# Keys grouped in column strips instead of row groups, and twice as many second-stage projections by the seven-product scheme

## The chip, the cores and the metric

The kernel runs on one core of a Trainium2 chip. The metric is the device time of one execution in microseconds; the time of a kernel is the median over several runs. The profile shows one execution on that core: TensorE (PE, with its weight loads as PEld), VectorE (DVE), ScalarE (ACT), GpSimd (POOL), and the queue on SyncE (SP), from which nearly all transfers are issued.

## What is computed

One layer of a neighbourhood-attention encoder over 2048 tokens of width 1024, which form a grid of 32 rows by 64 columns, with 16 heads of 64, all in float32:

```python
h = rmsnorm(x, g)
q, k, v, gate = split(h @ w_in, 4)
# each query at (row, col) sees the 8 x 16 keys of a window clipped to the grid
s = q . k / 8 + rpb[head, row offset, column offset]
o = softmax(s) . v
x = x + (o * silu(gate)) @ w_out
out = rmsnorm(x, norm_f)
```

## The kernel before

**Precision.** A float32 operand is split into a high and a low part in the reduced matmul format (`hi` and `lo`), and three products (high by high, high by low, low by high) stand for one. Splits are made in pairs, the high part by ACT and the low part by DVE.

**Projections.** `w_in` has 16 units of 256 columns, four for each of q, k, v and gate. Tokens come in four chunks of 512 (chunk c holds rows 8c to 8c+7). `stage_one` makes v for tokens 0 to 1023 (`values_of`, L531), then q, k and gate of all four unit numbers for chunks 0 and 1. It does this by `seven_products` (L411): a Strassen-like scheme that makes the 2 x 2 blocks of a unit (two halves of the columns by two chunks) from seven block products of 12 matmuls each, 84 in all, instead of 96. Its `ahead` forms the weight sums (L400) and their splits (L393 on ACT, L394 on DVE) six products ahead; `add` and `out_` (L422, L428, L430) put the blocks together from PSUM, and `give` stores them to DRAM. `stage_two` makes v for the other tokens (L531), then, again by `seven_products`, the units of `units_two` for chunks 2 and 3. All other units of chunks 2 and 3 (`halves`) are left to the generator `projections`, which makes 24 matmuls per group (`group`, L355, L357 and L359) as filler of the attention stage. When it is used up, the generator `outputs` (L1250, L1252, L1254) makes the output projection, as filler too, and after the attention.

**Attention.** `order` lists pairs of heads p by row groups T of eight query rows; each is done in two iterations, one for column blocks C = 0, 1 and one for 2, 3, with 128 queries a block (8 rows by 16 columns). `KEY_ROWS` and `KEY_COLS` give the keys a block can see: 11, 15 or 12 rows by 24 or 32 columns. Iteration i of the main loop issues, in this order: filler (`feed`, which has `amount[i]` matmuls to give and goes on for a while after the last event on ACT and DVE); `normalise(i-1)` (reciprocals on DVE L1004, scaling on POOL L1006); `turns(i-2)` (transposes L1011, copied out of PSUM by DVE L1036 and ACT L1035); `scores(i)` (L988; then maximum with the bias added on DVE L995, exponential on ACT L998); `values(i-2)` (L1056; in the second of the two iterations the product with the gate on DVE, L1070). `bias` (L970, POOL) adds mask and relative position bias for a new pair of heads or row type.

**Order of keys.** Keys of a block lie row by row. `blocks(T)` cuts them into groups of four rows: a group is 96 or 128 keys deep (72 or 96 for a last group of three rows), and a half of the queries (64 partitions) needs only those groups that its window touches. The products with the values need the values in the same order on partitions: `evac_v` stores v to `vd` in DRAM, `copy_v` (L946) copies it within DRAM into one array `vc` for each pair of heads and column block, and `load_v` (L938) loads one tile `vt` for each of the four column blocks of a pair and row group.

**Order of work.** The program is scheduled by hand: every instruction stands in the order of the source. Transfers and evacuations that may come later are put into `later` with a lag counted in matmuls (`store`, `due`). Pools have fixed numbers of buffers; `vp` (values, and landing places before) has four of 512 elements.

Of the kernel before, what the change touches and what calls it, by code (L numbers as in the profile page):

```python
# [43 lines left out]
def mask_table():  # L44
    out = []
    for t, (u0, u1) in enumerate(TYPE_ROWS):
        T = (0, 1, 3)[t]
        for c, (v0, v1) in enumerate(TYPE_COLS):
            C = (0, 1, 3)[c]
            qr = T * 8 + np.arange(8)[:, None, None, None]  # L50
            qc = C * 16 + np.arange(16)[None, :, None, None]
            kr = T * 8 + np.arange(u0, u1)[None, None, :, None]
            kc = C * 16 + np.arange(v0, v1)[None, None, None, :]
# [17 lines left out]
def build(ctx, tc, x, xr, xt, wg, rpb, w_out, n0, nf, masks, out):  # L71
# [7 lines left out]
    vd = [dram.tile([4, 4, GW, 8, 128], F32, name=f"vd{u}") for u in range(2)]  # L79
    vc = {(p, C): dram.tile([4 * (c1 - c0), 8, 128], F32, name=f"vc{p}_{C}")  # L80
          for p in range(NP) for C, (c0, c1) in enumerate(KEY_COLS)}
# [12 lines left out]
    vp = pool("vp", 4)  # L94
# [126 lines left out]
    units_two = [(k, j) for j in range(1) for k in "kqg"]  # L221
    halves = [(k, j, 1, c) for j in range(1, 4) for g in (("k", "q", "g") if j < 3 else ("k", "qg")) for c in (2, 3) for k in g]
# [98 lines left out]
    def give(kind, hp, c, t, psum=False):  # L321
# [19 lines left out]
        nc.scalar.activation(hi, t, AF.Copy)  # L341
        nc.vector.tensor_tensor(lo, t, hi.bitcast(F32), OP.subtract)
# [22 lines left out]
    def evac_v(u, t, p):  # L365
        v = ev([128, 512], F32, "v")
        nc.scalar.activation(v, p, AF.Copy, scale=rt[:, t:t + 1] if t < 8 else 1.0)
        dst = vd[u].rearrange("h r c g d -> g (r c) h d")[t // 2, t % 2 * 128:t % 2 * 128 + 128]
# [169 lines left out]
    uncopied = [[(p, C, h) for p in range(NP) for C in range(4)] for h in range(2)]  # L538

    def copies(h, n):  # L540
        for _ in range(n):
            if uncopied[h]:
                copy_v(*uncopied[h].pop(0))


    def stage_one():
        us = [(k, j) for j in range(4) for k in "kqg"]
        X1 = {f: [(xs([128, 512], F32R, "h"), xs([128, 512], F32R, "l")) for _ in range(4)]
              for f in ("B12", "B11", "B21", "B22")}
        spot = mkp([128, 3, 512], F32, "spot")  # L550
        land = {f: [p([128, n], F32, "land")[:, :512] for _ in range(4)]
                for f, p, n in (("x12", kp, 960), ("x22", qp, 512), ("x11", vp, 512))}
        land["x21"] = [spot[:, k] for k in range(3)] + [lp([128, 512], F32, "land")]
        slots = [(mp, 512)] * 6 + [(ep, 512)] * 2 + [(sp, 512)] * 2 + [(pa, 768)] * 2 + [(vp, 512)] * 4
# [23 lines left out]
        def also(n, i):  # L578
            m = n + len(us) - 1
            if m and i in (1, 3, 5):  # L580
                copies(0, 1)
# [27 lines left out]
            if n == 0:  # L609
# [16 lines left out]
                elif i == 3:  # L626
                    split_v(0, 1, 1)
                    L2["x12"] = [vp([128, 512], F32, "land") for _ in range(4)]
# [127 lines left out]
    def stage_two():  # L756
        x12, x11, x21 = L2["x12"], L2["x11"], L2["x21"]
        x22 = [qp([128, 512], F32, "land") for _ in range(4)]
        for k in range(4):
# [3 lines left out]
                 "T4": [(vp, 512)] * 4 + [(mp, 512)] * 2 + [(ep, 512)] * 2}  # L763

        def also(n, i):
            copies(1, 1)
# [21 lines left out]
        def pair(u, ts, *do):  # L788
            for b in range(4):
# [3 lines left out]
                if u and ts != (12,) and b % 2:  # L793
                    copies(1, 1)
# [167 lines left out]
    def bias(p, ty, cty):  # L962
# [3 lines left out]
        sh = lambda a: a.rearrange("p (u v) -> p u v", v=v1 - v0)  # L966
        for s in range(2):
# [3 lines left out]
                sh(t), E[p, s][:, u0 + 4:u1 + 4, v0 + 8:v1 + 8], sh(MK[0][:, m0:m0 + n]), OP.add)  # L971
# [3 lines left out]
    def scores(i):  # L975
# [5 lines left out]
        for C in cs:  # L981
# [3 lines left out]
            for m, (qq, kk) in enumerate(((qh, kh), (qh, kl), (ql, kh))):  # L985
                for s in range(2):
                    a = slice(s * 64, s * 64 + 64)
                    nc.tensor.matmul(pst[s], qq[a, qs], kk[a, :r1 - r0, c0:c1], start=(m == 0), stop=(m == 2))  # L988
# [19 lines left out]
    def turn(dst, i, C, s, blk, q0, nq):  # L1008
        g, lr, nr = blk[:3]
        w = width(C)  # L1010
        nc.tensor.transpose(dst[:nr * w], X[i, C][s][q0:q0 + nq, lr * w:(lr + nr) * w],  # L1011
                            ident[q0:q0 + nq, q0:q0 + nq])

    def split(T):
        bl = blocks(T)
        return [b for b in bl if b[4] == 128], [b for b in bl if b[4] == 64]

    def turns(i):
        p, T, cs = pairs[i]
        full, part = split(T)  # L1020
        halves_ = [full + [b for b in part if b[3] == 64 * h] for h in range(2)]
        for C in cs:
            t = PT[i, C] = pa([128, 768], F32, "pta")
            slots = t.rearrange("p (n h q) -> p h n q", h=2, q=64)
            ph = [bank(384, f"ph{h}") for h in range(2)]
            for j in range(3):
                for s in range(2):
                    for h in range(2):
                        if j < len(halves_[h]):
                            o = j * 128 + s * 64  # L1030
                            turn(ph[h][:, o:o + 64], i, C, s, halves_[h][j], 64 * h, 64)
# [364 lines left out]
```

## Time and profile before

| | us |
|---|---|
| median of 3 runs | 1085.62 (1084.97 to 1085.65) |
| the profiled execution, its own time | 1086.36 |
| its span, first to last instruction | 1084.5 |
| `seven_products` of stage one on PE, from the chain | 96.7 to 326.7 |
| `values_of` of stage two | 326.7 to 414 |
| `seven_products` of stage two and first filler | 414 to 478 |
| attention | 478 to about 1027 |

The page gives busy time, share of the span and number of instructions for each engine; matmuls overlap in the array, so that the records of PE are longer than the distance between their starts. A group of instructions is a line of the kernel with its engine, operation, tiles and shape, the count after an x, then busy us, mean ns of one, and the engine's idle time before them with what ended it. A row of the timeline has its start and length in us, and in brackets the idle time before it. Two more rows of interest, the transfers that the change takes out (KB each, median us from issue to landing):

```profile
vc<-vd SPq DMA_DIRECT2D x32, 256.0 KB, 4.4
...
vc<-vd SPq DMA_DIRECT2D x32, 192.0 KB
```

### The profile page before, as it was taken

What the parts mean: (1) busy time and instruction counts of PE and PEld (TensorE: products, weight loads), DVE (VectorE), ACT (ScalarE), POOL (GpSimd) and SP (SyncE); (2) the same over time, 40 slices, a digit from 0 to 9 for tenths busy, and PEclk for the clock granted to TensorE, in tenths of its full rate; (3) what the DMA queues carried; (4) which work ended last, traced back from release to release, by engine and by line L of the source; (5) the groups of instructions that cost most, each with busy time, mean ns of one, the idle gap of its engine ahead of it and who ended that gap; (6) DMA issues with size and microseconds to landing.
All of it is one profiled execution on the core that took longest, in us unless ns stands there. A gap on an engine that the chain in (4) does not pass through costs nothing.

```text
span 1084.5 us, 21929 instructions
## 1 busy us (share of the span) xinstructions
PE 1071.1 (99%) x7657; PEld 877.1 (81%) x7657; DVE 703.2 (65%) x1644; ACT 531.2 (49%) x1345; POOL 357.9 (33%) x474
## 2 busy tenths in 40 slices
PE   9999999999999999999999999999999999999997
PEld 6888888888888888887888888888888787888885
DVE  5376778778997535576555555664676786776643
ACT  7545334333434334346555555564576565665431
POOL 0000222312221000017545534444447656566200
PEclk9999999999999999999999999999999999999999
DMA  9633557574764366889868876886899787887442
GB/s 313 212 97 106 202 173 210 163 232 146 256 188 143 108 172 170 258 277 310 245 205 267 253 216 204 255 269 200 246 319 294 230 268 231 274 262 226 126 149 78
DMA packets 145901, 231.90 MB, mean 214 GB/s; under 512 B 13824, under 2 KB 61184, under 8 KB 145792
## 3 DMA queue, kind: packets, MB, share of 16 engines
q1 hardware_dynamic: 145648, 230.25, 68.2%
q8 instruction: 61, 1.00, 0.4%
q14 instruction: 48, 0.39, 0.1%
q10 hardware_dynamic: 144, 0.26, 0.1%
HBM read 171.73 MB, written 73.40 MB: 226 GB/s over the span
## 4 chain that ended last, share of the span: by engine, by line
PE 92%; DVE 3%; DMA 1%; ACT 1%; issue 1%; SPq 0%; POOL 0%; ACTq 0%; DVEq 0%; POOLq 0%
PE pp L411 23%; PE pv L531 16%; PE o L1056 8%; PE s L988 6%; PE pp L359 6%; PE pp L357 6%; PE pp L355 6%; PE po L1254 6%; PE po L1252 5%; PE po L1250 5%; PE ph L1011 5%; PE zp L1269 1%; DMA k_hi<-hi 1%; DMA land<-in_xt_dram 0%; DVE f L394 0%
## 5 line engine op out<-in xcount | busy, mean ns | idle before, releaser
L1006 POOL TENSOR_SCALAR x<-x,st 128x360 f32<-128x360 f32 (+5 forms) x256 | 143.0, 578 | 235.0 <-DVE st L1004 192.3
L970 POOL TENSOR_TENSOR em<-e,mk 128x480 f32<-128x480 f32 (+5 forms) x160 | 136.3, 886 | 138.3 <-DMA raw<-in_xt_dram 135.0
L998 ACT ACTIVATE x<-x,st 128x360 f32<-128x360 f32 (+5 forms) x256 | 151.8, 595 | 44.4 <-DVE st L995 44.4
L411 PE MATMUL pp<-h,f 128*128 128x512 f32 x480 | 155.4, 389 | 0.0
L430 POOL TENSOR_TENSOR tmp<-tmp,rb 128x512 f32<-128x512 f32 x36 | 58.9, 1637 | 270.6 <-DVE tmp L428 223.7
L411 PE MATMUL pp<-t,f 128*128 128x512 f32 x540 | 130.0, 390 | 0.3 <-DVE u L422 0.2
L995 DVE CUSTOM_DVE_ANT_0 x<-s,em 128x360 f32<-128x360 f32 (+5 forms) x256 | 124.0, 539 | 5.3 <-PE s L988 1.4
L411 PEld LDWEIGHTS pp<-t,f 128*128 128x128 f32 x540 | 101.2, 188 | 22.2 <-DVE u L422 1.2
L359 PE MATMUL pp<-h,w 128*128 128x512 f32 x288 | 115.1, 400 | 0.0
L357 PE MATMUL pp<-l,w 128*128 128x512 f32 x288 | 113.2, 393 | 0.0
L355 PE MATMUL pp<-h,w 128*128 128x512 f32 x288 | 113.1, 393 | 0.0
L1035 ACT ACTIVATE pta<-ph 96x256 f32<-96x256 f32 (+1 forms) x224 | 58.5, 333 | 104.3 <-PE ph L1011 104.3
L1036 DVE COPY pta<-ph 128x384 f32<-128x384 f32 (+3 forms) x128 | 60.7, 514 | 72.7 <-PE ph L1011 72.5
L411 PEld LDWEIGHTS pp<-h,f 128*128 128x128 f32 x480 | 90.1, 188 | 18.8
L1254 PE MATMUL po<-wol,gh 128*128 128x512 f32 x252 | 100.3, 398 | 0.0
L1252 PE MATMUL po<-woh,gl 128*128 128x512 f32 x252 | 98.9, 393 | 0.0
L1250 PE MATMUL po<-woh,gh 128*128 128x512 f32 x252 | 98.9, 392 | 0.0
L1056 PEld LDWEIGHTS o<-pta,vt 96*64 96x64 f32 (+2 forms) x1792 | 83.6, 137 | 17.2 <-issue 10.2
L1056 PE MATMUL o<-pta,vt 96*64 96x128 f32 (+4 forms) x1792 | 92.3, 254 | 1.4 <-DVE pta L1036 1.0
L411 PE MATMUL pp<-l,f 128*128 128x512 f32 x240 | 93.4, 389 | 0.0
L531 PE MATMUL pv<-wh,h 128*128 128x512 f32 x256 | 88.1, 390 | 0.0
L531 PE MATMUL pv<-wh,l 128*128 128x512 f32 x256 | 88.0, 389 | 0.0
(148 smaller groups left out, 1916.6 us busy)
## 6 DMA issues: line engine op xcount, KB each, us to landing
raw<-in_wg_dram SPq DMA_DIRECT2D x126, 256.0 KB, 5.1
e<-in_rpb_dram SPq DMA_DIRECT2D x54, 240.0 KB, 3.9
vt<-vc SPq DMA_DIRECT2D x64, 192.0 KB, 3.7
row<-in_xr_dram SPq DMA_DIRECT2D x32, 256.0 KB, 4.3
vd<-v SPq DMA_DIRECT2D x32, 256.0 KB, 3.0
k_hi<-hi SPq DMA_DIRECT2D x32, 256.0 KB, 2.6
k_lo<-lo SPq DMA_DIRECT2D x32, 256.0 KB, 3.8
vc<-vd SPq DMA_DIRECT2D x32, 256.0 KB, 4.4
```

The lines of the kernel that those rows point to most:

```text
L355: nc.tensor.matmul(p, wh[w, b][:, cols], hh[k, c], start=(k == 0), stop=False)
L357: nc.tensor.matmul(p, wh[w, b][:, cols], hl[k, c], start=False, stop=False)
L359: nc.tensor.matmul(p, wl[w, b][:, cols], hh[k, c], start=False, stop=(k == NK - 1))
L411: nc.tensor.matmul(B[n, P], t[:, int(m == 2), c], x[k][int(m == 1)], start=P in (1, 6, 5) and k == 0 and m == 0, stop=k == 3 and m == 2, s ...
L531: nc.tensor.matmul(ps[t], a[:, o], b, start=k == 0 and m == 0, stop=k == NK - 1 and m == 2)
L970: (nc.gpsimd if attending[0] or not s else nc.vector).tensor_tensor(sh(t), E[p, s][:, u0 + 4:u1 + 4, v0 + 8:v1 + 8], sh(MK[0][:, m0:m0 + n ...
L998: nc.scalar.activation(X[i, C][s], X[i, C][s], AF.Exp, bias=st[:, s:s + 1], scale=-1.0, accum_out=st[:, 2 + s:3 + s])
L1006: nc.gpsimd.tensor_scalar(X[i, C][s], X[i, C][s], st[:, 4 + s:5 + s], 0.5, op0=OP.mult, op1=OP.mult)
L1056: nc.tensor.matmul(o[s * 64:s * 64 + 64, C * 128 + q0:C * 128 + q0 + nq], vt[C][:k, g - g0_, s * 64:s * 64 + 64], t[:k, at:at + nq], start ...
L1250: nc.tensor.matmul(p, gh, woh[q, j], start=(i == 0), stop=False)
L1252: nc.tensor.matmul(p, gl, woh[q, j], start=False, stop=False)
L1254: nc.tensor.matmul(p, gh, wol[q, j], start=False, stop=(i == NK - 1))
```

## The change

Keys of a block are grouped into strips of eight columns by all its rows (88, 96 or 120 keys deep), three or four strips a block. So `blocks(T)` becomes `strips(C)`: which half of the queries needs a strip depends on the column block instead of the row group. The order of tokens in DRAM is changed on the host (within a row, column s x 8 + c lies at c x 8 + s), so that `load_v` gets one tile for all four column blocks of a pair and row group straight from `vd`, partition by (row, c), with the eight strips one after another. `vc` and its copies go. Masks, bias and the columns of the scores are laid out by strip; q, k and the gate are brought into or out of the new token order with strided views where they are evacuated or read. `turns` has one copy on each engine, since all strips of a block are equally deep. `vp` has two buffers of 1024 elements, of which `vh` hands out halves to the earlier stages.

`units_two` has six units instead of three, and `halves` six fewer pairs of chunk and unit; `amount` follows from this, eight matmuls more go to each of the first three iterations, and the debt that `feed` may run up is half an iteration's amount instead of 12.

```diff
-def blocks(T):
-    r0, r1 = KEY_ROWS[T]
+def strips(C):
     out = []
-    for g in range(r0 // 4, (r1 + 3) // 4):
-        halves = [h for h in range(2) if abs(2 * T + h - g) <= 1]
-        out.append((g, 4 * g - r0, min(4, r1 - 4 * g), halves[0] * 64, len(halves) * 64))
+    for s in range(KEY_COLS[C][0] // 8, KEY_COLS[C][1] // 8):
+        halves = [h for h in range(2) if abs(2 * C + h - s) <= 1]
+        out.append((s, s - KEY_COLS[C][0] // 8, halves[0] * 64, len(halves) * 64))
     return out
...
-    vp = pool("vp", 4)
+    vp = pool("vp", 2)
+    vhalf = []
+
+    def vh(shape, dt, nm):
+        if not vhalf:
+            t = vp([128, 1024], dt, nm)
+            vhalf.extend((t[:, :512], t[:, 512:]))
+        return vhalf.pop(0)
...
-    units_two = [(k, j) for j in range(1) for k in "kqg"]
-    halves = [(k, j, 1, c) for j in range(1, 4) for g in (("k", "q", "g") if j < 3 else ("k", "qg")) for c in (2, 3) for k in g]
+    units_two = [(k, j) for j in range(2) for k in "kqg"]
+    halves = [(k, j, 1, c) for j in range(2, 4) for g in (("k", "q", "g") if j == 2 else ("k", "qg")) for c in (2, 3) for k in g]
...
     def tiled(t):
-        return t.rearrange("p (r C c) -> p C r c", r=8, c=16)
+        return t.rearrange("p (r c s) -> p s r c", c=8, s=8)
     def blocked(t):
-        return t.rearrange("p (C r c) -> p C r c", r=8, c=16)
+        return t.rearrange("p (s r c) -> p s r c", r=8, c=8)
+    def by_place(t):
+        return t.rearrange("p (r c s) -> p r s c", c=8, s=8)
+    def by_column(t):
+        return t.rearrange("p (r s c) -> p r s c", s=8, c=8)
...
-        nc.scalar.activation(hi, t, AF.Copy)
-        nc.vector.tensor_tensor(lo, t, hi.bitcast(F32), OP.subtract)
+        nc.scalar.activation(by_column(hi), by_place(t), AF.Copy)
+        nc.vector.tensor_tensor(by_column(lo), by_place(t), by_column(hi.bitcast(F32)), OP.subtract)
...
-    def load_v(p, T, C):
+    def load_v(p, T):
         r0, r1 = KEY_ROWS[T]
-        g0_, g1_ = r0 // 4, (r1 + 3) // 4
-        c0, c1 = KEY_COLS[C]
-        def block():
-            VT[p, T, C] = t = vp([128, 4, 128], F32, "vt")
-            nc.sync.dma_start(t[:4 * (c1 - c0), :g1_ - g0_], vc[p, C][:, g0_:g1_])
-        return [block]
-
-    def copy_v(p, C, h):
-        must(*[("v", p // 4, t) for t in range(8 * h, 8 * h + 8)])
-        c0, c1 = KEY_COLS[C]
-        g = slice(512 * h, 512 * h + 512)
-        nc.sync.dma_start(vc[p, C].rearrange("(r c) g d -> c r (g d)", r=4)[:, :, g],
-                          vd[p // 4][p % 4].rearrange("r c g d -> c r (g d)")[c0:c1, :, g])
+        must(*[("v", p // 4, t) for t in range(r0 // 2, (r1 + 1) // 2)])
+        rows = vd[p // 4][p % 4].rearrange("(k s) d -> k s d", s=8)[8 * r0:8 * r1]
+        VT[p, T] = t = vp([128, 1024], F32, "vt").rearrange("p (s d) -> p s d", s=8)
+        nc.sync.dma_start(t[:8 * (r1 - r0)], rows)
...
-                    nc.tensor.matmul(pst[s], qq[a, qs], kk[a, :r1 - r0, c0:c1], start=(m == 0), stop=(m == 2))
+                    nc.tensor.matmul(pst[s], qq[a, qs], kk[a, :r1 - r0, c0:c1].rearrange("p r (s c) -> p s r c", c=8), start=(m == 0), stop=(m == 2))
...
             for h in range(2):
-                four = sum(b[2] == 4 for b in halves_[h])
-                k = 4 * width(C)
+                n = len(halves_[h])
                 put = (lambda o, i_: nc.scalar.activation(o, i_, AF.Copy)) if h else nc.vector.tensor_copy
-                put(slots[:k, h, :2 * four], ph[h][:k, :128 * four].rearrange("p (n q) -> p n q", q=64))
-                if four < len(halves_[h]):
-                    k = halves_[h][four][2] * width(C)
-                    put(slots[:k, h, 2 * four:2 * four + 2],
-                        ph[h][:k, 128 * four:128 * four + 128].rearrange("p (n q) -> p n q", q=64))
+                put(slots[:k, h, :2 * n], ph[h][:k, :128 * n].rearrange("p (n q) -> p n q", q=64))
...
-    amount = [early / 48] * 48 + [(384 - 30) / 18] * 18
+    first = 8
+    amount = [(early - 3 * first) / 48] * 48 + [(384 - 30) / 18] * 18
+    calm_debt = amount[0] / 2
+    for i in range(3):
+        amount[i] += first
...
-        while credit[0] > 0 or credit[0] > -12 and clock[0] - state["event"] < calm:
+        while credit[0] > 0 or credit[0] > -calm_debt and clock[0] - state["event"] < calm:
...
-        if 0 < i <= N:
-            p, T, cs = pairs[i - 1]
-            later_loads(load_v(p, T, cs[0]) + load_v(p, T, cs[1]), 0, 2)
+        if i % 2 == 0 and i < N:
+            load_v(*order[m])
```

More of the change, by code (lines that the diff above doesn't have):

```diff
@@ L78, in build @@
     sgd = [dram.tile([128, S], F32, name=f"sgd{p}") for p in range(NP)]
-    vd = [dram.tile([4, 4, GW, 8, 128], F32, name=f"vd{u}") for u in range(2)]
-    vc = {(p, C): dram.tile([4 * (c1 - c0), 8, 128], F32, name=f"vc{p}_{C}")
-          for p in range(NP) for C, (c0, c1) in enumerate(KEY_COLS)}
+    vd = [dram.tile([4, S, 128], F32, name=f"vd{u}") for u in range(2)]
     ogd = [dram.tile([128, 4, NP, 128], F32, name=f"ogd{T}") for T in range(4)]
@@ L627, in also @@
                     split_v(0, 1, 1)
-                    L2["x12"] = [vp([128, 512], F32, "land") for _ in range(4)]
+                    L2["x12"] = [vh([128, 512], F32, "land") for _ in range(4)]
                     for k in range(4):
@@ L1006, in normalise, with split @@
                 nc.gpsimd.tensor_scalar(X[i, C][s], X[i, C][s], st[:, 4 + s:5 + s], 0.5, op0=OP.mult, op1=OP.mult)
[L1008 to L1016, printed above, removed]
+    def split(C):
+        return [b for b in strips(C) if b[3] == 128], [b for b in strips(C) if b[3] == 64]
     def turns(i):
         p, T, cs = pairs[i]
-        full, part = split(T)
-        halves_ = [full + [b for b in part if b[3] == 64 * h] for h in range(2)]
+        k = 8 * (KEY_ROWS[T][1] - KEY_ROWS[T][0])
         for C in cs:
+            full, part = split(C)
+            halves_ = [full + [b for b in part if b[2] == 64 * h] for h in range(2)]
             t = PT[i, C] = pa([128, 768], F32, "pta")
@@ L1047, in values @@
         o = O[p, T]
-        g0_ = KEY_ROWS[T][0] // 4
-        vt = {C: VT.pop((p, T, C)) for C in cs}
+        vt = VT[p, T]
         for C in cs:
@@ L1065, in values @@
                 for s in range(2):
-                    product(C, s, blk, PT[i, C], 512 + s * 128 + blk[3], False, h == len(part) - 1)
+                    product(C, s, blk, PT[i, C], 512 + s * 128 + blk[2], False, h == len(part) - 1)
             del PT[i, C]
         if cs[1] == 3:
+            del VT[p, T]
             og = ev([128, 512], F32, "og")
```

53 lines of the change are left out of this document (22 added, 31 removed).

## The prediction

> **What bounds the kernel now.** I read the page's busy times and clock first, then the chain that ended last, then the matrix engine's waits, then stretches of the timeline.
>
> ```profile
> span 1084.5 us, 21929 instructions
> PE 1071.1 (99%) x7657; PEld 877.1 (81%) x7657; DVE 703.2 (65%) x1644; ACT 531.2 (49%) x1345; POOL 357.9 (33%) x474
> ...
> PEclk9999999999999999999999999999999999999999
> ...
> PE 92%; DVE 3%; DMA 1%; ACT 1%; issue 1%; SPq 0%; POOL 0%; ACTq 0%; DVEq 0%; POOLq 0%
> ```
>
> A busy PE is not yet a PE at its pace, so I look for the pace in the chain in order of time (start, length, what) and for gaps in the waits of PE from 482 us to 1025 us, the attention stage.
>
> ```profile
> 181.18 68.32 PE pp L411 x300
> 329.86 84.34 PE pv L531 x372
> ...
> PE o L1056 <- DVE pta L1036: 1.0, 3, 0.3
> PE s L988 <- DVE lo L342: 0.9, 1, 0.9
> PE s L988 <- ACT pta L1035: 0.9, 3, 0.4
> PE o L1056 <- ACT pta L1035: 0.3, 1, 0.3
> PE s L988 <- DVE y L1161: 0.2, 1, 0.2
> ```
>
> 84.34/372 is 0.227 us for one 128x512 product, and 68.32/300 is 0.228 us for those of the seven-product scheme, though each record is some 390 ns long: they overlap. In the attention stage PE waits 3.3 us in all of 543 us, and no wait names a transfer. So the kernel is a queue of PE work at full clock. An edit counts if it changes the number of 512-column products, their pace, or opens a gap.
>
> **Products removed and added.** `units_two` grows from three to six. Each of the three moved units cost 96 products by `group` (two outputs, two chunks, 24 each); by `seven_products` it costs 7 x 12 = 84.
>
> ```profile
> L355 PE MATMUL pp<-h,w 128*128 128x512 f32 x288 | 113.1, 393 | 0.0
> L411 PE MATMUL pp<-t,f 128*128 128x512 f32 x540 | 130.0, 390 | 0.3 <-DVE u L422 0.2
> ```
>
> L355, L357 and L359 go from 288 each to 192 each: 288 x 0.227 = 65.4 us leave the attention stage, where they are the filler between attention steps. 3 x 84 = 252 join L411: 252 x 0.227 = 57.2 us more in stage two. The difference is 36 products, **-8.2 us**. [...]
>
> **Transposes and products with the values.** Their counts do not change (1408 transposes, 896 products): before, the number for a pair went by the row group (20 or 24, and 24 or 32 recorded passes), now by the column block (always 22 and 28). Only the depth changes: 72, 96 or 128 becomes 88, 96 or 120.
>
> ```profile
> 650.60 0.92 PE L1011 MATMUL ph<-ident,x 64*128 64x64 f32 x24
> 652.66 1.56 PE L1056 MATMUL o<-pta,vt 128*64 128x128 f32 x32
> 659.81 0.91 PE L1011 MATMUL ph<-ident,x 64*96 64x64 f32 x24
> 661.94 1.56 PE L1056 MATMUL o<-pta,vt 96*64 96x128 f32 x32
> ```
>
> In one iteration the depth is 128, in the next 96, and the blocks last the same. Term: 0.
>
> **Scores.** L988 now reads the keys in runs of 8 columns instead of 24 or 32; no operand of before has runs so short. Nearest rows:
>
> ```profile
> L988 PE MATMUL s<-kt,qh 64*128 64x360 f32 x128 | 18.0, 346 | 0.0
> L988 PE MATMUL s<-kt,qh 64*128 64x352 f32 x64 | 11.1, 350 | 0.9 <-DVE lo L342 0.9
> ```
>
> 360 elements are 15 runs of 24, 352 are 11 runs of 32: more runs, no more time. I take 0; the other bound is a stream at half pace, and as L988 holds 6% of the chain (65 us), that is +65 us.
>
> **Vector, scalar and GpSimd work.** Three more units add 21 forms with two splits each, plus sums and outputs; 12 weight splits go on each of ACT and DVE, and the second copy of `turns` on ACT (96 instructions). DVE is nearest its limit at the end of stage one, where the scheme already runs twelve units. Windows by stretch first, then the busy time of L394 on DVE and L411 on PE up to 274.8 us, with counts:
>
> ```profile
> 269.00:298.00 29.00, 28.79 (x128) 23.48 (x127) 28.44 (x38) 11.35 (x21) 8.22 (x5) 1.00 0.79 257
> 414.00:478.00 64.00, 64.00 (x284) 52.97 (x283) 39.35 (x61) 20.44 (x36) 3.44 (x4) 1.00 0.81 251
> 501.00:618.00 117.00, 117.00 (x1112) 96.28 (x1110) 62.84 (x208) 65.06 (x205) 61.51 (x100) 1.00 0.80 252
> ...
> 0.00:274.80 274.80, 60.10 (x69) 1.00 0.60 187
> ...
> 0.00:274.80 274.80, 177.80 (x783) 146.98 (x784) 1.00 0.60 187
> ```
>
> (Columns: stretch, length, busy PE, PEld, DVE, ACT, POOL, clock, DMA share, GB/s.) Even with DVE at 28.44 of 29 us, 69 forms are done when PE is at 783/12, its 66th product: three products, 3 x 12 x 0.227 = 8.2 us in hand. Stage two loads DVE 39.35/64 = 61%. Term: 0 in both stages.
>
> The `by_place` and new `tiled` views read every eighth element, 32 bytes apart (L342's `lo`, L341's `hi`, the q outputs, `og` at L1070). The trace has only runs:
>
> ```profile
> L313 DVE TENSOR_TENSOR tmp<-pp,rb 128x512 f32<-128x512 f32 x8 | 5.5, 688 | 3.7 <-PE pp L411 3.7
> L315 DVE TENSOR_TENSOR tmp<-pp,rb 128x512 f32<-128x512 f32 x4 | 2.8, 688 | 1.2 <-PE pp L411 1.2
> L1070 DVE TENSOR_TENSOR og<-o,sgt 128x512 f32<-128x512 f32 x32 | 22.0, 687 | 4.2 <-PE pp L359 2.6 <-PE o L1056 1.1
> ```
>
> L315 reads 16-element runs at the 688 ns of the contiguous L313. I take 0 extra, and a second 0.69 us on each as the other bound. In stage one's last triple that is eight operations on DVE (four k, four q), 5.5 us, less than the 8.2 us in hand.
>
> GpSimd's `em` (L970) gets runs of 8 as well:
>
> ```profile
> L970 POOL TENSOR_TENSOR em<-e,mk 128x360 f32<-128x360 f32 x44 | 40.2, 935 | 0.0
> L970 POOL TENSOR_TENSOR em<-e,mk 128x352 f32<-128x352 f32 x15 | 13.9, 949 | 1.3 <-DVE st L995 1.3
> ```
>
> Again 15 runs cost no more than 11. POOL needs 61.51 us for the 14 iterations of 501 to 618 us, 4.4 us each; these shrink from 8.3 to about 6.9 us and still cover it.
>
> **Transfers.** Issues, with KB each and us to landing:
>
> ```profile
> vt<-vc SPq DMA_DIRECT2D x64, 192.0 KB, 3.7
> ...
> vt<-vc SPq DMA_DIRECT2D x32, 144.0 KB, 4.2
> ```
>
> The 64 copies vd to vc and the 128 loads of vt go; 32 loads of up to 480 KB come, two iterations ahead of their use. Nobody on PE waited for one, so the gain is 0 there. Does the denser stage still fit? 252 GB/s over 8.3 us are 2.1 MB an iteration; the vt loads of the first row group shrink from 2 x 192 + 2 x 144 = 672 to 352 KB in two iterations, 160 KB each, and some 6.5 fillers fewer take their weights and stores with them, about 25 KB each (estimate: 1 MB of weights per 96, 256 to 512 KB of stores per 24). That leaves 1.8 MB in 6.9 us, 257 GB/s, as now. On the SP queue a load of vt still waits for the products that free its buffer, but once in two iterations, not four times.
>
> **Shorter iterations.** The filler falls from 22 to 15.5 products an iteration, 1.48 us less cover, and unevenly: in the changed program 14 of the 48 iterations before the last row group have at most 11 fillers (down to 7), where before there were five. What has to fit beneath: maximum (L995), exponentials (L998), reciprocal (L1004), copies of the transposes (L1036, L1035), then the value products. An iteration of before with 11 fillers, on DVE and PE:
>
> ```profile
> 692.74 0.17 DVE L1004 RECIPROCAL st<-st 128x2 f32<-128x2 f32 x1 [0.54 <-ACT x L998]
> 694.43 1.02 DVE L1036 COPY pta<-ph 96x384 f32<-96x384 f32 x2 [1.52 <-PE ph L1011]
> 695.99 1.56 PE L1056 MATMUL o<-pta,vt 96*64 96x128 f32 x32
> ```
>
> The reciprocals end at 692.91, the copies start at 694.43 when PE has transposed: 1.52 us to spare, 6.7 fillers. So the point is 11 - 6.7, about 4 fillers, or 7 when one 0.69 us evacuation stands between. Seven fillers are just at the edge. Where the output's chain of small operations sits on DVE, gaps were seen:
>
> ```profile
> 855.40 0.71 PE L988 MATMUL s<-kt,qh 64*128 64x480 f32 x3 [0.45 <-ACT pta L1035]
> 890.88 1.56 PE L1056 MATMUL o<-pta,vt 96*64 96x128 f32 x32 [0.34 <-DVE pta L1036]
> ```
>
> Per short iteration the bounds are 0 (at 691 us) and 0.45 us; I take 0.17, half of the 0.34 of the one with 9 fillers: nine more of them make **+1.5 us** (0 to 14 x 0.45 = 6.3).
>
> **The start of attention.** The first pairs now have three longer iterations (`first`), and their keys are no longer those of the unit just stored.
>
> ```profile
> 494.02 0.67 PE L988 MATMUL s<-kt,qh 64*128 64x352 f32 x4 [0.94 <-DVE lo L342]
> 495.14 1.33 PE L1056 MATMUL o<-pta,vt 96*64 96x128 f32 x24 [0.29 <-DVE pta L1036]
> ```
>
> At most 1.2 us go; I take **-0.6 us**.
>
> **Sum.** -8.2 + 1.5 - 0.6 = -7.3 us. The profiled execution took 1086.36 us (span 1084.5 and 1.9 around it), 0.74 above the median of the runs, 1085.62; from it follow 1079.1 for its kind and **1078.3 us** for a median.
>
> **Rivals.** *The vector queue becomes the bound (slower).* Odd iterations carry `og` (0.69 us) and the split of the queries (0.69 us) on DVE as well, before the reciprocals. If each of the 24 odd iterations in the first 48 pays the 0.45 us of 855.40, that is 10.8 us: 1085.6 - 8.2 - 0.6 + 10.8 = 1087.6. It decides from 8.8/48 = 0.18 us lost per iteration on average. For it speaks that the saving is a small difference of two large terms; against it the 1.52 us to spare above. *Strided reads cost double.* Then `og` delays the reciprocals by another 0.69 us; over the odd ones of the 14 short iterations 7 x 0.69 = 4.8 us: 1083.1. For it: no row excludes it; against: 16-element runs were free. [...] *Short runs slow the scores:* 1078.3 + 65 = 1143 at half pace, break-even at 13% slower; the two rows of L988 speak against. *The lighter queues remove the waits too:* -8.2 - 3.3 = 1074.1; for it, ACT loses 96 copies; against it, only 1.2 of the 3.3 us name ACT. That the change does not remove the products is out: they are counted.
>
> **Chances.** Forecast, 1074 to 1083: 0.60. All waits gone or better: 0.06. Strided reads or part of the gain given back, 1083 to 1086: 0.15, half of it under the bound. Vector queue, 1086 to 1092: 0.15. Scores: 0.04. About 0.2%, 2.2 us, can be told from no change. Faster 0.73, same 0.08, slower 0.19. The range, 1074 to 1088, reaches over the part that gives back the gain and into the vector queue; the forecast's own is 1074 to 1083.
>
> **What would show it.** Right: L411 with 504 products in stage two at 0.228 us, the start of attention some 57 us later, iterations of about 6.9 us, L988 blocks as long as before, L1070 and L342 near 690 ns. Wrong: PE waiting for L1036 or L1035 in most iterations; L1070 or L342 far above 690 ns; a longer block of scores; L411 waiting for L394.

## The result, and the profile after

| | before | after |
|---|---|---|
| median, us | 1085.63 (1084.97 to 1086.54) | 1091.67 (1090.01 to 1092.86) |
| ratio to before | 1 | 1.0054, interval 1.0036 to 1.0072 |
| span of the profiled execution, us | 1084.5 | 1091.1 |

The change makes the kernel 6 us slower, where 7.3 us less were forecast, and the time lies outside the range of 1074 to 1088. The profiled execution of after is the longest of its four (1092.86 us). First its page, busy times and instructions.

```profile
span 1091.1 us, 21499 instructions
...
PE 1073.2 (98%) x7621; PEld 875.0 (80%) x7621; DVE 763.6 (70%) x1680; ACT 541.7 (50%) x1258; POOL 365.6 (34%) x474
```

PE has 36 products less, as counted. What stands out is DVE: 60 us more work than before. The chain in order of time (start, length, what) tells in which stage the time is; each of these links has its counterpart in the prediction's account or just below it.

```profile
337.14 84.34 PE pv L542 x372
421.48 111.53 PE pp L422 x492
```

In the profile of before, the same two links read:

```profile
329.86 84.34 PE pv L531 x372
414.20 54.41 PE pp L411 x240
```

The values of stage two start 337.14 - 329.86 = 7.3 us late, so stage one, whose products are the same in both kernels, has lost 7.3 us. Stage two runs at its pace: 111.53 - 54.41 = 57.1 us for 252 products, 57.2 were forecast. The waits of PE in after (for whom, us in total, times, longest) name the loser in stage one; before had 0.2 us on the first of these lines:

```profile
PE pp L422 <- DVE u L433: 4.4, 4, 1.8
PE s L977 <- DVE pta L1018: 2.0, 2, 1.3
...
PE s L977 <- DVE lo L353: 0.5, 1, 0.5
```

L433 is `add`, the sum of a product with the kept first one. No wait names a weight's split (L405). These waits are 4.2 of the 7.3 us (4.4 less the 0.2 of before), and 1.7 are a dip, a stretch of 3.41 us at a clock of 0.50 behind one of them (183.70 to 187.11 us, last section); 1.4 us aren't accounted for by single rows. That the dip is a part of its own shows in the profile of e2, one of the experiments below, where stage one does the same work with the same 4.4 us of waits and at full clock (1.00 from 180 to 190 us):

```profile
96.14 68.28 PE pp L422 x300
...
334.87 84.34 PE pv L542 x372
```

From the first of the seven products at 96.14 to the values at 334.87 are 238.7 us; before took 329.86 - 96.72 = 233.1. So the waits and what goes with them cost 5.6 us, and the dip makes 7.3 of it in the profile of after. The groups of after on DVE and ACT show what became of the operations with new views (mean ns is the number after the comma):

```profile
L1048 DVE TENSOR_TENSOR og<-o,sgt 128x512 f32<-128x512 f32 x32 | 38.3, 1197 | 1.8 <-PE o L1032 1.8
...
L353 DVE TENSOR_TENSOR lo<-tmp,hi 128x512 fp32r<-128x512 f32 x22 | 28.2, 1280 | 6.9 <-ACT hi L352 6.1
...
L353 DVE TENSOR_TENSOR lo<-pp,hi 128x512 fp32r<-128x512 f32 x10 | 6.9, 686 | 3.0 <-ACT hi L352 3.0
...
L326 DVE TENSOR_TENSOR tmp<-pp,rb 128x512 f32<-128x512 f32 x4 | 4.6, 1142 | 0.0
```

```profile
L352 ACT ACTIVATE hi<-tmp 128x512 fp32r<-128x512 f32 x22 | 26.6, 1208 | 39.4 <-POOL tmp L441 27.1 <-DVE tmp L439 9.2 <-DVE tmp L324 2.0
```

The two forms of L353 step over the data in the same way, every eighth element; one reads `tmp` from SBUF, the other `pp` from PSUM. Out of PSUM the step is free (686 ns here, and 686 ns for `lo` out of PSUM in before, without a step), out of SBUF the operation takes almost twice as long: 1280 against 681 ns for `lo`, 1208 against 630 for `hi`, as these rows of before show:

```profile
L342 DVE TENSOR_TENSOR lo<-tmp,hi 128x512 fp32r<-128x512 f32 x19 | 12.9, 681 | 3.2 <-ACT hi L341 3.2
```

```profile
L341 ACT ACTIVATE hi<-tmp 128x512 fp32r<-128x512 f32 x19 | 12.0, 630 | 35.2 <-POOL tmp L430 27.3 <-DVE tmp L428 4.2 <-DVE tmp L313 2.0
```

Third, the blocks of scores. The windows of both kernels from 470 to 1040 us, for the products of tile `s` alone (stretch, length, time with such a product under way and their number, clock, DMA share, GB/s), before and then after:

```profile
470.00:1040.00 570.00, 91.04 (x768) 1.00 0.78 243
```

```profile
470.00:1040.00 570.00, 99.80 (x768) 1.00 0.73 227
```

8.8 us more for the same 768 products. From start to start of all records of PE in the two traces, the account is: stage one +7.3, stage two +57.1, filler in attention -65.9, scores with the waits before them +7.1, transposes -1.1, all else +2.3; together +6.8, for a span longer by 6.6. A second dip, from 849.26 us on (clock 0.50), falls on products with the values and outputs and is 1.7 of the 2.3.

### The profile page after: what moved, and what is told of

Same layout as the page of the kernel before. It is cut to its first block, busy times and chain, and to the rows that moved or that the text cites. A ratio compares the mean times of both kernels' runs of the same rounds, so it can differ in the third digit from the quotient of the medians.

```text
span 1091.1 us, 21499 instructions
## 1 busy us (share of the span) xinstructions
PE 1073.2 (98%) x7621; PEld 875.0 (80%) x7621; DVE 763.6 (70%) x1680; ACT 541.7 (50%) x1258; POOL 365.6 (34%) x474
## 4 chain that ended last, share of the span: by engine, by line
PE 62%; DVE 4%; ACT 3%; issue 2%; DMA 1%; SPq 0%; POOL 0%; DVEq 0%; ACTq 0%
PE pp L422 11%; PE pv L542 8%; PE o L1032 7%; PE s L977 6%; PE po L1232 5%; PE po L1230 5%; PE po L1228 5%; PE ph L1014 4%; PE pp L370 4%; PE pp L366 3%; PE pp L368 3%; ACT x L987 2%; DMA kt<-k_lo 0%; DVE land L499 0%; DVE tmp L439 0%
## 5 line engine op out<-in xcount | busy, mean ns | idle before, releaser
L422 PE MATMUL pp<-h,f 128*128 128x512 f32 x576 | 186.4, 389 | 0.0
L422 PE MATMUL pp<-t,f 128*128 128x512 f32 x648 | 158.1, 393 | 4.4 <-DVE u L433 4.4
L422 PEld LDWEIGHTS pp<-t,f 128*128 128x128 f32 x648 | 122.2, 189 | 32.4 <-DVE u L433 7.0
L422 PEld LDWEIGHTS pp<-h,f 128*128 128x128 f32 x576 | 108.1, 188 | 22.5
L422 PE MATMUL pp<-l,f 128*128 128x512 f32 x288 | 112.0, 389 | 0.0
L1032 PEld LDWEIGHTS o<-pta,vt 120*64 120x64 f32 (+2 forms) x1792 | 84.3, 138 | 18.8 <-issue 14.3
L1018 DVE COPY pta<-ph 120x384 f32<-120x384 f32 (+5 forms) x128 | 62.6, 515 | 45.8 <-PE ph L1014 45.2
L1017 ACT ACTIVATE pta<-ph 120x384 f32<-120x384 f32 (+5 forms) x128 | 52.2, 458 | 85.0 <-PE ph L1014 84.9
L1032 PE MATMUL o<-pta,vt 120*64 120x128 f32 (+5 forms) x1792 | 93.2, 256 | 0.6 <-DVE pta L1018 0.3
L977 PE MATMUL s<-kt,qh 64*128 64x480 f32 (+5 forms) x512 | 86.7, 378 | 3.2 <-DVE pta L1018 2.0
L542 PE MATMUL pv<-wl,h 128*128 128x512 f32 x256 | 87.9, 389 | 0.0
L405 DVE TENSOR_TENSOR f<-raw,f 128x512 fp32r<-128x512 f32 x90 | 68.0, 756 | 18.7 <-ACT f L404 18.7
```

What stands on the lines that cost most here:

```text
L405: nc.vector.tensor_tensor(t[:, 1], src, t[:, 0].bitcast(F32), OP.subtract)
L422: nc.tensor.matmul(B[n, P], t[:, int(m == 2), c], x[k][int(m == 1)], start=P in (1, 6, 5) and k == 0 and m == 0, stop=k == 3 and m == 2, s ...
L542: nc.tensor.matmul(ps[t], a[:, o], b, start=k == 0 and m == 0, stop=k == NK - 1 and m == 2)
L977: nc.tensor.matmul(pst[s], qq[a, qs], kk[a, :r1 - r0, c0:c1].rearrange("p r (s c) -> p s r c", c=8), start=(m == 0), stop=(m == 2))
L1032: nc.tensor.matmul(o[s * 64:s * 64 + 64, C * 128 + q0:C * 128 + q0 + nq], vt[:k, strip, s * 64:s * 64 + 64], t[:k, at:at + nq], start=firs ...
```

## The experiments

The theory after the result has three parts: (A) strided reads of SBUF fill DVE's queue in stage one, and `add` comes late; (B) runs of eight columns slow the scores; (C) the shorter iterations cover less. The rivals to each are named in the expectations. Times are medians, each beside the runs of before on the same chip. There were twelve runs, of eleven kernels (e7 ran twice).

| run | us | before, us | ratio, interval |
|---|---|---|---|
| e1_no_strides | 1087.38 | 1085.47 | 1.0017, 1.0001 to 1.0032 |
| e2_og_plain | 1091.15 | 1085.47 | 1.0055, 1.0040 to 1.0070 |
| e3_long_runs | 1086.90 | 1085.47 | 1.0015, 1.0004 to 1.0026 |
| e4_six_units_only | 1080.99 | 1085.47 | 0.9963, 0.9950 to 0.9976 |
| e5_three_units | 1098.87 | 1085.98 | 1.0119, 1.0104 to 1.0134 |
| e6_order_out_of_psum | 1084.95 | 1085.98 | 0.9993, 0.9983 to 1.0003 |
| e7_keys_by_strip | 1080.08 | 1085.98 | 0.9946, 0.9931 to 0.9961 |
| e8_even_filler | 1087.99 | 1085.98 | 1.0019, 1.0010 to 1.0029 |
| e9_roots_after_scores | 1076.21 | 1086.77 | 0.9908, 0.9894 to 0.9921 |
| e10_before_short_runs | 1090.39 | 1086.77 | 1.0037, 1.0023 to 1.0050 |
| e7_again | 1080.93 | 1086.77 | 0.9950, 0.9938 to 0.9963 |
| e11_roots_kept | 1080.89 | 1085.81 | 0.9952, 0.9939 to 0.9966 |

### The layout and the six units, each alone: e4, e5

e4 is before with `units_two`, `halves`, `amount` and `calm_debt` of after, and nothing else. e5 is after with these four as before.

```diff
-    units_two = [(k, j) for j in range(1) for k in "kqg"]
+    units_two = [(k, j) for j in range(2) for k in "kqg"]
```

> The kernel before with six units by seven products in stage two and the new amounts of filler, all else as before (row groups, copies in DRAM, 16-element views). Theory S: 36 products fewer, no stride: 1085.6 - 8.2 and up to 2 us of short iterations, 1078 to 1080; stage one ends at 326.7 us. Rival C: the attention stage loses 7 us here too, 1084 to 1086. Rival M: stage two gets slower than 0.228 us a product.

> The changed kernel with three units in stage two again and the amounts of filler of before: the new layout alone. If the parts add up (strided SBUF reads 7 us in stage one, short runs of keys 4 to 5 us in the scores, nothing from shorter iterations), 1085.5 + 11 to 12 = 1096 to 1098. If short runs cost only beneath a short filler, or the stage-one loss comes with the six units, 1088 to 1093.

The six units alone gain: 0.9963, some 4 us, though not the 7.3 forecast. The layout alone loses 13 us (1.0119). Put together, six units take 1098.87 - 1091.67 = 7.2 us off e5. So the change is a gain and a loss, and the loss is the layout's. The gain is 4.5 us on the old layout and 7.2 on the new; each is known no better than to 1.5 us, so whether the two parts simply add up isn't shown. What the six units don't gain shows in e4's waits and in its windows of scores:

```profile
PE o L1056 <- DVE pta L1036: 1.5, 3, 0.9
PE s L988 <- ACT pta L1035: 1.2, 3, 0.7
PE s L988 <- DVE lo L342: 0.6, 1, 0.6
PE s L988 <- DVE y L1161: 0.4, 2, 0.3
PE o L1056 <- ACT pta L1035: 0.3, 1, 0.3
...
PE s L988 <- DVE pta L1036: 0.2, 1, 0.2
```

```profile
470.00:1040.00 570.00, 93.12 (x768) 1.00 0.79 249
```

The waits come to 4.2 us, 0.9 more than the 3.3 of before, and the scores have 2.1 us more under way. From start to start they are 3.0 us dearer and the outputs 0.7: 3.7 us where the prediction put 1.5 (C). Its bounds, 0 to 6.3, hold it. Why the scores take 2.1 us more under way isn't shown.

### The strides: e1, e2, e6

e1 makes all strided views plain; q, k and the gate then stay in the order in which they come, and pair with other keys. e2 does so only where `og` reads the gate.

```diff
-        return t.rearrange("p (r c s) -> p s r c", c=8, s=8)
+        return t.rearrange("p (s r c) -> p s r c", r=8, c=8)
...
-        return t.rearrange("p (r c s) -> p r s c", c=8, s=8)
+        return t.rearrange("p (r s c) -> p r s c", s=8, c=8)
```

> The changed kernel with the views that step over every eighth element (`by_place`, `tiled`) replaced by plain ones of the same shape: q, k, the gate and the factors rb are not brought into the new order of tokens, all else stays, the instructions too. Theory S (SBUF reads 32 bytes apart take twice as long on DVE and ACT, fill DVE in stage one and delay the additions that free the banks): `lo` of k, `og` and the q operations come back from 1.14-1.28 us to about 0.69 us, the wait of the seven products for the additions goes, values of stage two start at 326.7 us instead of 334.0, and the time falls by 7 us and a little more from the attention stage: 1083, at most 1085. Rival C (too little filler over the chain of the softmax): stage one as S says or not, the attention stage still takes 491 us. Rival M (more forms, sums and splits as such): 1090 or more.

> The changed kernel with only the gate's view at the product with the attention output made plain (the gate is applied in another order of tokens). Theory S for the attention stage: `og` falls from 1.20 to 0.69 us, and if its extra 0.5 us is what lengthens the chain before the copies of the transposes, some 2 to 4 us come back: 1088 to 1090. Rivals C and P (short runs in the scores): no change, 1091 to 1092. Stage one is as before this edit in all cases.

e2 is where after is: 1091.15 beside 1091.67. Its 32 products with the gate take 688 ns again, and nothing on PE's path changes. e1 takes 4 us off, less than was expected: DVE's busy time falls from 763.6 to 729.0 us, the wait of L422 for L433 to before's 0.2, and stage one is whole again (97.53 to 330.63, or 233.1 us as in before). Its profiled execution, the longest of eight (1091.3), has its excess in the attention stage, with a mean clock of 0.99 from 470 to 1040 us where e6 has 1.00 (last section). How the wait arises is seen in DVE's timeline of after (start, length, what):

```profile
171.52 1.15 DVE L353 TENSOR_TENSOR lo<-tmp,hi 128x512 fp32r<-128x512 f32 x1
...
175.06 2.18 DVE L353 TENSOR_TENSOR lo<-tmp,hi 128x512 fp32r<-128x512 f32 x1
...
180.22 1.12 DVE L353 TENSOR_TENSOR lo<-tmp,hi 128x512 fp32r<-128x512 f32 x1
...
182.47 0.67 DVE L433 TENSOR_TENSOR u<-pp,p 128x512 f32<-128x512 f32 x1
```

and the same stretch in e1:

```profile
174.70 0.67 DVE L353 TENSOR_TENSOR lo<-tmp,hi 128x512 fp32r<-128x512 f32 x1
...
179.44 0.69 DVE L353 TENSOR_TENSOR lo<-tmp,hi 128x512 fp32r<-128x512 f32 x1
...
181.25 0.68 DVE L433 TENSOR_TENSOR u<-pp,p 128x512 f32<-128x512 f32 x1
```

Both lists run in the order of the source. The splits of k ahead of `add` are 0.4 to 1.5 us longer (a split of a weight beside them, which takes 1.77 us in e1 and 0.70 in after, gives 1.1 us back). The `add` before this one came 0.5 us earlier than in e1 (165.10 against 165.57 us), and this one comes 1.2 us later, at 182.47 instead of 181.25. On PE, the next product needs the bank that `add` reads: in `seven_products`, products 6, 7 and 4 are accumulated in one bank (L411 with `start` only at P = 6), as are 1 and 2, and 5 and 3. PE in after:

```profile
183.19 4.61 PE L422 MATMUL pp<-t,f 128*128 128x512 f32 x12 [1.81 <-DVE u L433]
...
302.68 3.02 PE L422 MATMUL pp<-t,f 128*128 128x512 f32 x12 [1.48 <-DVE u L433]
```

The splits of weights (L405) stand in the same queue and are still done well ahead; what is late is the reading of a bank, with one product's 2.7 us (12 x 0.227) between its filling and its next use.

e6 keeps the order of tokens of after and computes all of it, but makes every change of order where an operation reads PSUM anyway (`keep`, `add`, `out_`, the first evacuation); SBUF is read in order.

```diff
+    def order_of(kind):
+        return (by_column, by_place) if kind == "k" else (blocked, tiled)
...
-            nc.vector.tensor_tensor(U[n, i], B[n, P], U[n, 1], OP.add)
+            lay, of = order_of(us[n][0])
+            nc.vector.tensor_tensor(lay(U[n, i]), of(B[n, P]), lay(U[n, 1]), OP.add)
```

> The changed kernel with the new order of tokens made where a result is first read out of PSUM (q, k and gate sums, and two copies of the factors rb), so that no operation reads SBUF in steps; the scores keep their short runs. Theory S, PSUM reads in steps at full speed (the 686 ns of `lo` from PSUM): stage one ends at 326.7 us, all of these operations at about 0.69 us, time as in the run without strides, 1086 to 1088. Rival: the steps cost on the PSUM side or on the write side as well, stage one stays 5 to 7 us late, 1091.

Stage one is whole again. The chain of e6 and its splits of k:

```profile
329.58 84.34 PE pv L552 x372
413.93 111.53 PE pp L430 x492
```

```profile
L361 DVE TENSOR_TENSOR lo<-tmp,hi 128x512 fp32r<-128x512 f32 x22 | 15.0, 682 | 5.2 <-ACT hi L360 5.0
```

329.58 against 329.86 of before, and 0.9993 for the whole: the loss of stage one comes from the strided reads of SBUF, (A), 5.6 us by itself and 7.3 with the dip of the clock behind a wait. The products and their number, the transfers and the copies of `turns` are as in after.

### The runs of eight: e3, e10, e7

e3 is after with the scores' keys read as before, in runs of 24 or 32 columns, so that the columns are in another order than the mask's. e10 is before with the keys read in runs of eight, likewise at odds with the mask.

```diff
-                    nc.tensor.matmul(pst[s], qq[a, qs], kk[a, :r1 - r0, c0:c1], start=(m == 0), stop=(m == 2))
+                    nc.tensor.matmul(pst[s], qq[a, qs], kk[a, :r1 - r0, c0:c1].rearrange("p r (s c) -> p s r c", c=8), start=(m == 0), stop=(m == 2))
```

> The changed kernel with the keys of the scores read row by row again, in runs of 24 or 32 columns instead of 8 (the scores are then in another order than mask, bias and values). Rival P (short runs slow the moving operand): the 768 matmuls of the scores fall from 93.6 us, start to start, to about 87 us, and the time to 1085 or 1086. Theory S and rival C: the scores stay at about 93 us and the time at 1091 to 1092.

> The kernel before with one edit: the scores read each block of keys strip by strip, in runs of 8 columns (the scores are then in another order than mask, bias and values). Filler, units and row groups stay. If short runs slow the moving operand by themselves, the 768 matmuls of the scores go from 86.5 us to about 92 us and the time from 1085.6 to 1090 to 1092. If they cost only beneath a short filler, the time stays within 1 us of 1085.6.

The same windows of tile `s`, in e3 and then in e10:

```profile
470.00:1040.00 570.00, 94.78 (x768) 1.00 0.74 229
```

```profile
470.00:1040.00 570.00, 96.86 (x768) 1.00 0.78 244
```

Long runs take 99.80 - 94.78 = 5.0 us out of after, short ones put 96.86 - 91.04 = 5.8 us into before; in the medians 4.8 and 3.6 (1.0037, that is 2.5 to 5.4). From start to start, with the waits, it is 93.6 - 89.9 = 3.7 and 90.6 - 86.5 = 4.1 us. So the one line at fault is shown from both sides, at 4 to 5 us. One of its groups in e10:

```profile
L988 PE MATMUL s<-kt,qh 64*128 64x360 f32 x128 | 19.6, 371 | 0.0
```

371 ns where before has 346, quoted in the prediction: 45 runs instead of 15 for 360 columns, so 25/30 = 0.8 ns a run; for 480 columns it is 429 against 414 ns with 45 runs more, 0.3 ns a run, so there is no one price. The two rows that the prediction compared differ by four runs; by the higher price they would be 3 ns apart, less than what else differs between them.

e7 is e6 with the keys in DRAM strip by strip, so that the scores read them without a step.

```diff
-    k_hi = [dram.tile([128, S], F32, name=f"k_hi{p}") for p in range(NP)]
+    k_hi = [dram.tile([128, 8, S // 8], F32, name=f"k_hi{p}") for p in range(NP)]
...
-                    nc.tensor.matmul(pst[s], qq[a, qs], kk[a, :r1 - r0, c0:c1].rearrange("p r (s c) -> p s r c", c=8), start=(m == 0), stop=(m == 2))
+                    nc.tensor.matmul(pst[s], qq[a, qs], kk[a, c0 * (r1 - r0):c1 * (r1 - r0)], start=(m == 0), stop=(m == 2))
```

> As e6, and the keys are stored in DRAM strip by strip, so that the scores read them in one run (360 or 480 elements long); in exchange the transfers of keys have pieces of 256 to 480 bytes. Theories S and P together: scores at 1.33 us a block or less, 1087.4 - 4.8 = 1082.6, between 1081 and 1084. Rival: the small pieces make the keys late, scores wait for transfers, 1086 or more.

> The kernel of e7 once more, on the same chip as e9 and with more rounds, so that the two can be compared: 1079 to 1081 again.

0.9946, and on another chip 0.9950: e7 leaves nothing of the layer out and beats both kernels, by 5.9 and 5.8 us against before. The 1081 to 1084 expected were counted from e1's median; from e6's 1084.95 the same 4.8 us lead to 1080.15. Its windows of scores, beside 100.55 us in e6:

```profile
470.00:1040.00 570.00, 94.77 (x768) 1.00 0.82 229
```

The DMA share rises from 0.73 to 0.82 with loads in eight pieces, and PE waits for none of them. e4, with the layout of before, is at 0.9963; the intervals overlap, so no worth of the new layout itself can be told.

### The iterations: e8, e9, e11

What the short iterations still lose was sought in e4 and e7. e8 is e4 without the overrun in `feed`, so that each iteration gets its 15 or 16 products.

```diff
-        feed(a * 0.55, 8)
+        feed(a * 0.55)
```

> Row groups with six units (e4) without the overrun of the filler: 15 or 16 products in each of the first 48 iterations instead of 7 to 24. If the short iterations are what e4 misses of its 8.2 us, 1078 to 1080. If the average cover is, or the overrun was needed to let ACT and DVE catch up, 1081 to 1086.

6 us worse than e4 (1.0019 beside 0.9963). Its costliest wait:

```profile
PE s L988 <- DVE y L1161: 3.0, 3, 1.6
```

That is also beyond the 1081 to 1086 expected. The overrun seems to put filler where DVE and ACT are late and to take it where they aren't. An even share is worse, so the short iterations that the prediction counted are not by themselves where time is lost.

One gap remains in e7's profile, in the iterations in which outputs run. POOL, DVE and PE there, in order of time:

```profile
833.51 5.49 POOL L969 TENSOR_TENSOR em<-e,mk 128x360 f32<-128x360 f32 x6
...
837.40 0.80 DVE L1169 SCALAR_TENSOR_TENSOR st<-st 128x1 f32<-128x1 f32 x1
...
839.05 0.16 DVE L1171 SCALAR_TENSOR_TENSOR st<-st 128x1 f32<-128x1 f32 x1
...
839.32 0.22 DVE L1003 RECIPROCAL st<-st 128x2 f32<-128x2 f32 x2
839.45 0.87 DVE L1028 COPY pta<-ph 120x256 f32<-120x256 f32 x2
...
839.91 0.70 PE L987 MATMUL s<-kt,qh 64*128 64x480 f32 x3 [1.53 <-DVE pta L1028]
```

The root of a finished output row, eight operations on one column, stands ahead of the reciprocals, and those ahead of the copy that PE waits for. While POOL makes `em` (to 839.0), those that read two tiles (L1168 to L1170) take 0.8 to 0.9 us, after it 0.16; the three ahead of them, with one tile to read, take 0.15 to 0.20 under `em` too. e9 puts the root off to the first half of an iteration.

```diff
         def root():
+            if state.get("tail"):
+                store(("y", n), 2, root)
+                return
+            store(("y", n), 12, scale)
+            store(("y", n), 32, send)
...
-        store(("y", n), 24, scale)
-        store(("y", n), 44, send)
```

> As e7, and the eight small operations on DVE that make the reciprocal root of an output row (`root`) no longer run between a pair's filler and its transposes, but after the maxima, in the next filler. If the remaining loss of the shorter iterations is this chain ahead of the copies of the transposes (block of scores 3.2 us instead of 1.3 at 835 us in e7), the blocks of iterations 33 to 47 come to below 2 us and 2 to 3 us come back: 1077 to 1078.5. If it is something else on DVE (operations with two SBUF inputs held up while POOL makes em), no change beyond 1 us: 1079.5 to 1080.5.

1076.21, but e9 leaves out the scaling and the store of the last output rows, whose turn comes after the last call of `due`. From the last product of the outputs to the end of the span it takes 1074.7 - 1070.2 = 4.5 us, e7_again 1079.1 - 1071.5 = 7.6: 3.1 us of its gain are work not done. e11 does that work, with scale 8 and send 24 products after the root.

```diff
-    due(1e9)
+    while later:
+        due(1e9)
```

> e7_again (ratio 0.995 to before) with the root of a finished row (eight small operations on DVE, `finish`) put off to the first half of an iteration, and with the scaling and the store of all rows, the last ones too, which e9 leaves out. Theory: the root ahead of the reciprocals and copies is a part of what the shorter iterations cost; then the blocks of scores take some 88.0 us as in e9 (88.6 in e7_again, 91.0 in e7), the last two output rows end as in e7 (8.2 us after the last product), and the time is 1076.2 + 3.1 = 1079.3, ratio 0.993 (0.992 to 0.994). Rival: all of e9's gain was the tail left out; then it takes what e7 takes, ratio 0.995 (0.994 to 0.996). A second rival: the scaling, now later than the root, holds buffers of the output longer and PE waits for them: 0.997 or more.

0.9952: what e7 takes. The rival by which e9's gain was the tail holds as far as it can be told, and the root's place is no cure. e11's profiled execution, the longest of its five (1084.6), has its longest wait elsewhere:

```profile
PE s L987 <- DVE y L1149: 2.6, 3, 1.7
```

It is for L1149, an evacuation of the outputs in the same queue, on which e7_again's profile shows no wait as long. With the root moved, another operation is the late one. Why e11 and e9 differ by 4.7 us where the work left out is 3.1 is open: the lags differ too, and no run separates them. So is the rest of (C) in e4 and e7, some 2 to 4 us, which no experiment removed.

## Why the prediction was wrong, by its steps

**Products removed, -8.2: right.** 252 products more in stage two, at 111.53/492 = 0.2267 us each, and 65.9 us less filler, -8.8 in all: the pace of 227 ns held.

**"Term: 0 in both stages": the step that failed first, +7.3 us** (5.6 without the dip of the clock). The slack was read off the weights' splits: 69 forms done at PE's 66th product, so three products or 8.2 us in hand. That is a stock that the queue fills ahead; nobody waits for it as long as it isn't empty. The tight place in the same queue is `add`, which must read a bank before PE may write it again, with one product, 2.7 us, for it and all that stands before it. The extra cost of the strided views had been bounded rightly (a second 0.69 us; 0.45 to 0.6 measured on DVE) and was then set against the wrong slack. The busy share misled as well: the account looked at the last triple, where DVE was busy 28.44 of 29 us, but the longest wait, 1.8 us at 183, lies in a stretch where DVE was busy 46.69 of 57 us (154 to 211 us in after). Of the prediction's own signs, a split far above 690 ns and longer scores came; L411 waiting for L394 did not.

**Strided views taken as runs: wrong.** L315, from which "0 extra" came, reads `rb` in runs of 16 elements out of SBUF and the product out of PSUM. Neither is a lone element in SBUF every 32 bytes. The rival of strided reads had the price right and the place wrong: it put it on `og` in the iterations, where e2 shows that it costs nothing (1091.15 us beside 1091.67).

**Scores, 0: wrong, +4 to 5 us.** The bounds, 0 and 65 us, held it. Two rows with 11 and 15 runs are no evidence for 45 or 60; the rival's break-even of 13% didn't apply, since the loss came on top of another.

**Shorter iterations, +1.5: mis-sized.** 3.7 us in e4, where they stand alone; this holds the start of attention too. There, -0.6 was put; the wait for L353 is 0.5 us where it was 0.9, so -0.4.

**Values, `em` and transfers, 0: right; transposes: 1.1 us better.** The same 1408 transposes take 44.1 us from start to start where they took 45.2. `em` takes 139.1 us on POOL in all its forms where it took 138.5, and no wait of PE names a transfer.

**Chances.** Two of the unknown costs, strides and runs, came at once. They were weighed as rivals that exclude each other, but they come from one layout and add up. With what the runs measured, the sum for the profiled execution is -8.8 (products) + 5.6 (strides) + 4.1 (runs) + 3.7 (shorter iterations) - 1.1 (transposes) + 3.4 (two dips of the clock) = +6.9, beside a span longer by 6.6 and a median higher by 6.0. No term of the prediction stood for the dips. That 1091.67 falls into the 1086 to 1092 of the vector-queue rival (0.15) is luck: it put the queue's delay into the odd iterations of attention, but PE's waits in attention are 3.4 us in after and were 3.3, and it had no loss in the scores.

## What to carry to other kernels

Read the slack of a queue at the operation that another engine needs soonest (here the reading of a PSUM bank that is written again one product, 2.7 us, later), not at work that the same engine does ahead; an operation made longer delays what stands behind it in the queue (here `add`, at 182.47 us instead of 181.25). A new order of data was free here where PSUM is evacuated (686 ns for `lo` with the step and without); laid down there, it let later reads of SBUF run through, by vector operations (`lo` 682 ns in e6 instead of 1280) and as a matmul's moving operand (scores 94.77 us in e7 instead of 100.55 in e6). If a layout only pays by what another edit brings, time the two apart. An unknown cost with bounds of 0 and 65 us deserves a row with runs as short as the new ones, or a chance to match.

## What the runs showed of the hardware

**The clock was halved for 3.41 us behind a wait of 1.81 us, but not behind each such wait.** After the wait of 1.81 us at 183.19 above, the windows of after (PE, PEld, DVE, ACT and POOL busy, then the clock) read:

```profile
180.00:183.70 3.70, 1.89 (x9) 1.27 (x8) 3.67 (x8) 0.00 (x0) 0.00 (x0) 1.00 0.76 232
183.70:187.20 3.50, 3.50 (x10) 2.68 (x10) 2.85 (x5) 1.68 (x3) 0.00 (x0) 0.52 0.60 183
```

From 183.70 to 187.11, 3.41 us, the clock is 0.50. The twelve products take 4.61 us, where those at 302.68 take 3.02, so the wait and the dip together cost 1.81 + 1.59 = 3.4 us. e3 has the same wait (1.84) and no dip:

```profile
183.70:187.20 3.50, 3.50 (x17) 2.89 (x16) 3.37 (x5) 2.23 (x4) 0.00 (x0) 1.00 0.58 177
```

In after, the second dip (849.26 to 852.67, clock 0.50) stands behind a wait of 1.29 us at 847.95, and behind the 1.48 us at 302.68 the clock stays at 1.00. In the 3.41 us ahead of the two dips PE stood idle for 53 and 38%. So the length of the wait alone doesn't decide, and what does isn't shown. e5 has a clock of 0.57 from 184.50 to 188.50 us. The mean clock of the profiled execution is 0.995 in e1, 0.996 in after, e5, e8 and e11, 0.997 in e7_again, and 0.998 or 0.999 in before and the other seven. The dips may be why some kernels spread wider (e1 from 1084.3 to 1091.3, e11 from 1079.8 to 1084.6): the mean clock of e1's shortest execution is 0.998 and of its longest 0.995, but no run tests that.

**A split on DVE took 3.83 us beside POOL's `em`, and 0.68 us ahead of it.** In e7 a weight's split that takes 0.68 us at 754.45 takes 3.83 us at 759.97, and ends at 763.80, 0.55 us after POOL's `em` (763.25):

```profile
754.45 0.68 DVE L184 TENSOR_TENSOR wol<-raw,woh 128x512 fp32r<-128x512 f32 x1
...
757.75 5.50 POOL L969 TENSOR_TENSOR em<-e,mk 128x360 f32<-128x360 f32 x6
...
759.97 3.83 DVE L184 TENSOR_TENSOR wol<-raw,woh 128x512 fp32r<-128x512 f32 x1 [1.13 <-ACT woh L183]
```

Both inputs of the split lie in SBUF. The maximum (L994), which reads the scores out of PSUM, takes 0.53 us both before `em` (from 757.25) and beside it (from 757.71). The split beside `em` took 3.2 us longer than the one ahead of it.
